# A weight tile place kept from the input stage, expert rows written back pair by pair, and a rearranged tail in a one-core transformer layer

## The chip, the core and the metric

The kernel runs on one core of a Trainium2 chip. The metric is device time in microseconds of one execution; the number compared is the median of repeated executions. One execution was recorded by the hardware profiler, and all rows below come from it.

## What is computed

One layer over 512 tokens of width 1024, all in float32: a modulated RMS norm, one wide input projection into a retention branch and a long convolution branch, a gated merge of both, an output projection with a residual, and then a mixture of experts. The experts hold most of the weights:

```python
h2 = modulate(rms_norm(x, norm2_g[layer]), sh2, sc2)
x = x + gt2 * moe_ffn(h2.reshape(-1, D_MODEL), *moe_args).reshape(x.shape)
return rms_norm(x, final_norm_g)

# moe_ffn: top-1 of 4 groups, top-2 of its 8 experts, and for each of 32 experts
def expert_block(args):
    xblk, e = args
    return (jax.nn.silu(xblk @ w1[e]) * (xblk @ w3[e])) @ w2[e]
```

Each of the 32 experts has `w1` and `w3` of 1024 x 512 and `w2` of 512 x 1024: 6 MB, 192 MB in all. That many bytes have to pass from HBM into the core once.

## The kernel before

The kernel works through the layer in stages. The first half (to about 548 us) is projections, retention and convolution; their weights are split into two parts on ScalarE and VectorE (`halved`), so TensorE makes three products for one. The normed tokens, eight tiles `hT` of [128, 2, 512], are an operand of every input projection; the last to read them is the second gate group, `gh` of `merge_group(1)`. After it come two more groups of that merge, `ho` (products with `hy_w_o`) and `ro` (with `ret_w_o`), and then the output projection (`w_out`), the residual and the router.

The second half is the expert stage. Experts are taken in 16 pairs. Each pair has a capacity of 64 tokens per expert, so a pair fills the 128 columns: expert 0 of the pair in the lower 64 partitions of a PSUM place, expert 1 in the upper. For a pair, TensorE does two `ga` and two `up` steps (`up_half`, L1536 to L1543, with `w1` and `w3`), the hidden product on ScalarE and VectorE (`hidden`), a transpose (`turned`, L1551) into `hT`, and two `y` steps (`down`, L1559) with `w2`. The result is scaled, split into `yh` and `yl`, and brought back to token order by products with the choice matrix `cmb` (`combine`, `add`, L1577 to L1590): for each of four token tiles and two halves of the width, the products are summed in PSUM and VectorE adds them to `xmid`.

Weights come in tiles of 1 MB, 12 to a pair: `plan` lists the 192 sources in the order of use, `sequence` the order of loading, and `ahead(n)` issues loads on SP, whose queue is worked in order. A tile goes to one of `NR` = 12 places of a ring (`ew`), or to a borrowed place (`loans`): work tiles of the expert stage that aren't needed yet (`cmb`, `hh`, `hT`, `y`, for tiles 6, 7, 10, 11), the tiles `xm` of the residual, and three spare ones (`xe0`, `xe1`, `xf`). From tile 16 on the pattern repeats every 16 tiles. A load waits until the products that read the place's last tile are done.

TensorE's order is written by hand in the expert stage (`tensor_order`); the order on SP, VectorE, ScalarE and GpSimd (POOL) is found by a planner, except in the tail (`with tc.manual_schedule()`), where all engines follow the text.

The loop over `g` in range(7) does two pairs per turn. The even pair's turn has `add(parts, places[:4])`, `turned`, `add(parts, places[4:])`, where `parts` holds the two pairs before; the odd pair adds nothing, but for `g == 6`. Pairs 14 and 15 stand behind the loop with their sums placed by hand: `fin` holds the first half of the width for four token tiles, `fin2` the second. In the last block the first half is added to `xmid` on VectorE, squared on ScalarE and multiplied by the final norm's gain on POOL (L1895 to L1899), and `leave` (from L1861) makes the norm, scales and sends out, two of the four rows on POOL (L1878).

Of the kernel before, what the change touches and what calls it, by code (L numbers as in the profile page):

```python
# [29 lines left out]
OV = 10  # L30
OA = 4
NA, NB, NC, NR, NW, NH = 12, 33, 4, 12, 2, 3
# [5 lines left out]
XE, XF = 12, 2  # L38
# [135 lines left out]
def body(es: ExitStack, tc: tile.TileContext, d, out, dump=None):  # L174
# [46 lines left out]
    rw = pa.tile([128, 8, 64], F32, name="rw")  # L221
    t1b = ExitStack()
# [649 lines left out]
    def start():  # L872
# [236 lines left out]

    def merge_group(ch):  # L1110
# [26 lines left out]

    gr, gh, ho, ro = merge_group(0)
# [17 lines left out]
    weave(ho, rest)  # L1156
    weave(ro, rest)
    run(rest)
    t1b.close()
# [10 lines left out]

    plan = []
    for p_ in range(16):
        for kc in range(2):
            for wt in ("w1", "w3"):
                for e in range(2):
                    plan.append(d[wt][2 * p_ + e, :, 4 * kc:4 * kc + 4, :].rearrange("p a b -> p (a b)"))
        for kc in range(2):
            for e in range(2):
                plan.append(d["w2"][2 * p_ + e, kc].rearrange("p a b -> p (a b)"))


    def borrow(pool, tag, bufs, units):
        def tile_():
            w = pool().tile([128, units, 512], F32, name="xw" + tag, tag=tag, bufs=bufs)
            return [w[:, u] for u in range(units)], w.rearrange("p a b -> p (a b)")
        return tile_

    lent_xm = [borrow(lambda: r2, "xm", 4, 2)] * 2
    wk_ = lambda: wk
    loans = {6: [borrow(wk_, "cmb", 4, 1)] * 4, 7: [borrow(wk_, "hh", HH, 1)] * 2 + [borrow(wk_, "hT", 2, 1)] * 2,  # L1190
             10: [borrow(wk_, "y", 4, 2)] * 2, 11: [borrow(wk_, "y", 4, 2)] * 2}
    sequence = [i for i in range(NR + len(loans)) if i not in loans] + list(LO)
    early_tiles = len(sequence)
    sequence += range(early_tiles, len(plan))

    loans.update((i, lent_xm) for i in range(early_tiles, len(plan) - 6)
                 if (i - early_tiles) % (NR + 4) < 2 and not 12 * OV + 8 <= i < 12 * OV + 8 + OA + 8)
    loans.update((i, [borrow(wk_, "xe0", 1, 2), borrow(lambda: late, "xe1", 1, 2)]) for i in range(early_tiles, len(plan) - 6)
                 if (i - early_tiles) % (NR + 4) == XE)
    loans.update((i, [borrow(wk_, "xf", 1, 4)]) for i in range(early_tiles, len(plan) - 6)  # L1200
                 if (i - early_tiles) % (NR + 4) == XF)
    PIECES = {len(plan) - 6: ((0, 2), (2, 3), (3, 4)), len(plan) - 4: ((0, 2), (2, 4)),
              len(plan) - 2: ((0, 2), (2, 3), (3, 4))}
    ready, lent = {}, {}
    issued, taken = [0], [0]

    def borrowed(src, places, queue=S):
        units = []
        for u, w in places:
            c0 = 512 * len(units)  # L1210
            queue.dma_start(w, src(slice(c0, c0 + 512 * len(u))))
            units += u
        return units

    def ahead(n):

        while issued[0] < min(n, len(plan)):
            i = sequence[issued[0]]
            src = plan[i]
            issued[0] += 1  # L1220
            if i in loans:
                if i < early_tiles and not lent:

                    lent.update((j, [place() for place in loans[j]]) for j in AL)
                ready[i] = borrowed(lambda c: src[:, c], lent.pop(i, None) or [place() for place in loans[i]])
                continue
            if i in PIECES:

                both = [ring_.tile([128, 4, 512], F32, name="ew", tag="ew") for e in range(2)]
                for a, b in PIECES[i]:  # L1230
                    for e, w in enumerate(both):
                        S.dma_start(w[:, a:b], plan[i + e].rearrange("p (a b) -> p a b", b=512)[:, a:b])
                for e, w in enumerate(both):
                    ready[i + e] = [w[:, u] for u in range(4)]
                issued[0] += 1
                continue
            w = ring_.tile([128, 2048], F32, name="ew", tag="ew")
            S.dma_start(w, src)
            ready[i] = [w[:, 512 * u:512 * u + 512] for u in range(4)]
# [50 lines left out]
    def prefetch():  # L1290
        for i in range(NR):
            yield
            ahead(i + 1)

    run(out_group(0, lambda o: [out_tile(o[m], m) for m in range(4)]))
    early, pre = early_steps(), prefetch()
# [406 lines left out]
    for g in range(7):  # L1703
# [7 lines left out]
        if g == 0:  # L1711
# [221 lines left out]
```

## Time and profile before

| | us |
|---|---|
| median of 3 runs (1096.97 to 1098.73) | 1098.47 |
| the profiled execution | 1098.42 |
| its span | 1096.8 |
| TensorE (PE) busy | 1056.1 |
| VectorE (DVE) busy | 580.1 |
| ScalarE (ACT) busy | 333.6 |
| bytes moved by DMA | 289.22 MB |

A reader begins with the slices of the span: in which stretch the DMA engines are full and in which TensorE has slack. Then come the waits of SP, which tell whether a stream of loads is held by its rate or by the places it loads into, and only then the order of instructions on TensorE in the stretch that matters. A share of busy time over the whole span says little here, since its two halves have different limits.

### The profile page before, as it was taken

The numbers are of one execution on the slowest core, as the hardware profiler recorded it, in microseconds if no ns is written. First come the engines' busy times: TensorE is split into PE (matmuls) and PEld (weight loads), VectorE is DVE, ScalarE is ACT, GpSimd is POOL, SyncE is SP. The second block draws the span as 40 slices with busy tenths as digits, with TensorE's granted clock in tenths as the row PEclk, the third lists the DMA queues.
The fourth block names the chain that finished last, engine by engine and source line by source line (L and its number), as shares of the span: only waits on it lengthen the run. The fifth ranks groups of instructions, "written<-read, shape, count | busy, mean of one in ns | idle before, by whom it ended". The sixth has DMA issues, their size and how long they took to land. (4 is left out here: it accounts for less than half of the span.)

```text
span 1096.8 us, 13058 instructions
## 1 busy us (share of the span) xinstructions
PE 1056.1 (96%) x4960; PEld 671.8 (61%) x4960; DVE 580.1 (53%) x1036; ACT 333.6 (30%) x582; POOL 49.2 (4%) x75
## 2 busy tenths in 40 slices
PE   9999999999999999999999999999998989999995
PEld 5667888877778777878788634444443534344332
DVE  4788895775475768976534443434331424334214
ACT  3676442445533554333324111101010110201012
POOL 0100000000000000000002000000000000000002
PEclk9999999999999999999998999999999999999998
DMA  7933444111122117785299989999999999999992
GB/s 278 293 110 97 134 135 132 58 58 58 58 86 68 55 42 272 249 270 187 81 404 409 363 324 419 416 417 418 416 417 418 415 419 416 417 418 417 417 398 87
DMA packets 64585, 289.22 MB, mean 264 GB/s; under 512 B 8196, under 2 KB 10372, under 8 KB 45062
## 3 DMA queue, kind: packets, MB, share of 16 engines
q1 hardware_dynamic: 59558, 274.50, 65.0%
q0 software_dynamic: 4960, 13.84, 3.7%
q8 instruction: 40, 0.66, 0.2%
q14 instruction: 27, 0.22, 0.1%
HBM read 288.05 MB, written 4.19 MB: 266 GB/s over the span
## 5 line engine op out<-in xcount | busy, mean ns | idle before, releaser
L198 DVE TENSOR_TENSOR wL<-raw,wH 128x512 fp32r<-128x512 f32 x142 | 97.0, 687 | 116.2 <-ACT wH L197 107.5
L197 ACT CAST wH<-raw 128x512 fp32r<-128x512 f32 x142 | 87.9, 621 | 206.4 <-PE ro L202 33.7
L1542 PE MATMUL up<-ew,xgm 128*64 128x512 f32 x440 | 118.5, 594 | 9.3 <-DMA ew<-w 9.3
L1548 DVE TENSOR_TENSOR hh<-hh,up 128x512 f32<-128x512 f32 x16 | 11.0, 687 | 170.1 <-PE up L1542 170.1
L1542 PE MATMUL ga<-ew,xgm 128*64 128x512 f32 x344 | 93.8, 594 | 4.9 <-DMA ew<-w 4.9
L1567 PE MATMUL y<-ew,hT 128*64 128x512 f32 x360 | 92.8, 595 | 1.9 <-DVE hT L1556 1.9
L1542 PEld LDWEIGHTS up<-ew,xgm 128*64 128x64 f32 x440 | 36.6, 137 | 76.4 <-issue 56.2
L1542 PEld LDWEIGHTS ga<-ew,xgm 128*64 128x64 f32 x344 | 29.6, 137 | 46.8 <-issue 36.8
L1492 ACT ACTIVATE xr<-xr,rs 128x512 f32<-128x512 f32 x15 | 10.8, 722 | 145.6 <-DMA xr<-rows,idx 145.5
L1567 PEld LDWEIGHTS y<-ew,hT 128*64 128x64 f32 x360 | 30.3, 137 | 40.4 <-issue 35.3
L1590 DVE TENSOR_TENSOR xmid<-xmid,co 128x512 f32<-128x512 f32 x60 | 40.5, 687 | 19.6 <-PE co L1582 19.1
L1547 ACT ACTIVATE hh<-ga 128x512 f32<-128x512 f32 x16 | 9.6, 598 | 122.7 <-PE ga L1542 117.3
L197 ACT CAST yh<-yv 128x512 fp32r<-128x512 f32 x30 | 18.5, 618 | 86.5 <-DVE yv L1573 75.8
L1582 PE MATMUL co<-yh,cmb 128*128 128x512 f32 x108 | 43.9, 406 | 0.0
L1573 DVE SCALAR_TENSOR_TENSOR yv<-y,wsl,gt 128x512 f32<-128x512 f32 x30 | 22.5, 749 | 38.3 <-PE y L1567 35.6
L1582 PE MATMUL co<-yl,cmb 128*128 128x512 f32 x108 | 42.4, 392 | 0.0
L342 DVE SCALAR_TENSOR_TENSOR acc<-adaw,scT,acc 128x1024 f32<-128x1024 f32 x28 | 35.7, 1282 | 11.4 <-DMA adaw<-ada 11.3
L1491 DVE TENSOR_SCALAR xr<-xr,rs 128x512 f32<-128x512 f32 x15 | 7.3, 487 | 51.9 <-DMA xr<-rows,idx 51.9
L1485 POOL DMA_INDIRECT xr<-rows,idx x15 | 15.4, 1029 | 359.8 <-DVE wsl L1532 348.3
L198 DVE TENSOR_TENSOR yl<-yv,yh 128x512 fp32r<-128x512 f32 x30 | 20.7, 691 | 17.4 <-ACT yh L197 17.3
L1497 ACT ACTIVATE xgm<-xg,sh2c,am2c 128x256 f32<-128x256 f32 (+1 forms) x36 | 16.6, 538 | 36.3 <-PE xg L1510 34.2
L1582 PEld LDWEIGHTS co<-yh,cmb 128*128 128x128 f32 x108 | 20.3, 188 | 11.5 <-issue 4.1
(486 smaller groups left out, 2385.9 us busy)
## 6 DMA issues: line engine op xcount, KB each, us to landing
ew<-w SPq DMA_DIRECT2D x141, 1024.0 KB, 17.4
raw<-w_in SPq DMA_DIRECT2D x52, 512.0 KB, 3.6
xwxm<-w SPq DMA_DIRECT2D x40, 512.0 KB, 13.8
adaw<-ada SPq DMA_DIRECT2D x32, 512.0 KB, 6.3
xwxf<-w SPq DMA_DIRECT2D x11, 1024.0 KB, 15.0
xwxe<-w SPq DMA_DIRECT2D x20, 512.0 KB, 18.7
adaw<-ada SPq DMA_DIRECT2D x32, 256.0 KB, 6.3
raw<-ret_w_o SPq DMA_DIRECT2D x8, 512.0 KB, 3.9
```

Of the source, the lines that this page charges most:

```text
L197: A.copy(h, src)
L198: V.tensor_tensor(out=l, in0=src, in1=f(h), op=ALU.subtract)
L342: V.scalar_tensor_tensor(out=acc[i], in0=w, scalar=scT[:, k, 0:1], in1=acc[i], op0=ALU.mult, op1=ALU.add)
L1485: G.indirect_dma_start(out=xr[j], out_offset=None, in_=rows, in_offset=bass.IndirectOffsetOnAxis(ap=idx, axis=0), bounds_check=511, oob_is ...
L1492: A.activation(xr[j][:, 512:1024], xr[j][:, 512:1024], AF.Copy, scale=rs)
L1497: A.activation(o, p, AF.Identity, bias=sh2c[:, k:k + 1], scale=am2c[:, k:k + 1])
L1542: T.matmul(ab_[i][64 * e:64 * e + 64], xg[k][:, c0 + 64 * e:c0 + 64 * e + 64], w[e][q], start=(k == 0), stop=(k == 7))
L1548: V.tensor_tensor(out=hh, in0=hh, in1=ab_[1], op=ALU.mult)
L1567: T.matmul(y_[kc][64 * e:64 * e + 64], hT_[:, 128 * k + 64 * e:128 * k + 64 * e + 64], w[e][k], start=(k == 0), stop=(k == 3))
L1573: V.scalar_tensor_tensor(out=yv, in0=y_[n], scalar=wsl, in1=gt2[:, ns], op0=ALU.mult, op1=ALU.mult)
L1582: T.matmul(p, cmb[:, 128 * t:128 * t + 128], y[j][:, ns], start=(start and i + j == 0), stop=(stop and i == len(parts) - 1 and j == 1))
L1590: V.tensor_tensor(out=xmid[:, t, ns], in0=xmid[:, t, ns], in1=p, op=ALU.add)
```

## The change

- `NR` goes from 12 to 8. The tokens `hT` of the first half get a pool of their own, `hw`, that stays open; weight tiles 0 to 3 and then four of every 16 tiles (offset `XH` = 3) are loaded into it, each tile as two places and so as two transfers of 512 KB.
- `plan`, `sequence`, `loans` and `ahead` move ahead of the merge stage, and `prefetch(4)` issues the first four tiles between the steps of `ho` and `ro` in `merge_group(1)`.
- In pair 0, scaling and transposing pair 1's tokens and the choice matrix of the next two pairs move from behind `down` to ahead of `turned`.
- Each pair is written back during the next: `add` in both halves of the loop, with one pair in `parts`.
- Up to the overflow branch (`a < OV`) no more than 12 x 10 + 8 = 128 tiles are asked for.
- In the tail, `started` brings the residual into PSUM by a product with the identity ahead of the sums. Pair 14's first half gets it for four token tiles; the second half's sums of pair 14 stand at other places in pair 15; two of the four sums of `y0` move behind the last `y` products; the multiplication by the gain moves from POOL to VectorE and reads PSUM; the scaling of rows 0 and 1 moves from POOL to ScalarE; all rows leave first half first.

```diff
-NA, NB, NC, NR, NW, NH = 12, 33, 4, 12, 2, 3
+NA, NB, NC, NR, NW, NH = 12, 33, 4, 8, 2, 3
-XE, XF = 12, 2
+XE, XF, XH = 12, 2, 3
+    hw = es.enter_context(tc.tile_pool(name="hw", bufs=1, side="right", reuse_waits="tile"))
...
-            hl = pb.tile([128, 2, 512], F32R, name="hT", tag="hT", bufs=8)
+            hl = hw.tile([128, 2, 512], F32R, name="hT", tag="hw", bufs=8)
...
+    loans.update((i, [borrow(lambda: hw, "hw", 8, 2)] * 2) for i in range(4))
+    period = NR + 8
+    sequence = [i for i in range(NR + len(loans)) if i not in LO] + list(LO)
...
+    loans.update((i, loans[0]) for i in range(early_tiles, len(plan) - 6) if XH <= (i - early_tiles) % period < XH + 4)
...
+    def prefetch(n):
+        for i in range(n):
+            yield
+            ahead(issued[0] + 1)
...
-    weave(ho, rest)
-    weave(ro, rest)
+    pre = prefetch(4)
+    weave(ho, rest, pre)
+    weave(ro, rest, pre)
     run(rest)
+    run(pre)
     t1b.close()
...
             hh = hidden(ab_)
+            scaled(rs[1], 1)
+            run(token_columns(xg, [1], 128))
             now = []
...
+            gt, more = rows_of(1)
+            run(more)
             hT_ = turned(hh)
...
-        parts = []
-        ahead(12 * a + early_tiles + 20)
-        parts.append((now[0][0], down(hT_, now[0][1], ahead_weights)))
+        ahead(min(12 * a + early_tiles + 20, 12 * OV + 8) if a < OV else 12 * a + early_tiles + 20)
+        parts = [(now[0][0], down(hT_, now[0][1], ahead_weights))]
...
         hh = up(a + 1, xg)
-        if g == 6:
-            add(parts, places)
-            parts = []
+        add(parts, places)
...
-        parts.append((now[1][0], down(hT_, now[1][1], ahead_weights)))
+        parts = [(now[1][0], down(hT_, now[1][1], ahead_weights))]
...
+    def started(p, parts, t, n, residual=True):
+
+        if residual:
+            T.matmul(p, ident, xmid[:, t, cols[n]], start=True, stop=False)
+        combine(parts, t, n, p, not residual, False)
...
+    p = bank("hT")
+    fin, fin2 = [bank("fin") for t in range(3)], []
+    started(fin[0], parts, 0, 0)
+    some(step, 1)
     hh = hidden(ab_)
+    started(fin[1], parts, 1, 0)
+    started(fin[2], parts, 2, 0)
     hT_ = turned(hh, p)
     ahead(len(plan))
-    y = down(hT_, now[0][1], ahead_weights, lambda: combine(parts, 2, 0, fin[2], True, False))
     fin.append(bank("fin"))
-    combine(parts, 3, 0, fin[3], True, False)
+    started(fin[3], parts, 3, 0)
+    y = down(hT_, now[0][1], ahead_weights)
...
-    some(step, 2)
+    some(step, 1)
+    fin2.append(bank("fin", "acc"))
+    T.matmul(fin2[0], ident, xmid[:, 0, cols[1]], start=True, stop=False)
     more_sums(yn[0], 0, fin[0])
     more_sums(yn[0], 1, fin[1])
     some(step, 1)
     more_sums(yn[0], 2, fin[2])
     more_sums(yn[0], 3, fin[3])
...
-    second_half()
-    second_half()
-    some(step, 1)
+    more_sums(yn[1], 0, fin2[0])
+    some(step, 2)
     hh = hidden(ab_)
     early_table(AF.Sqrt, hh[:, 0:1])
+    fin2.append(bank("fin", "acc"))
+    T.matmul(fin2[1], ident, xmid[:, 1, cols[1]], start=True, stop=False)
     hT_ = turned(hh, bank("hT", "acc"))
+    more_sums(yn[1], 1, fin2[1])
...
         A.copy(yh, yv)
+        fill()
         V.tensor_tensor(out=yl, in0=yv, in1=f(yh), op=ALU.subtract)
...
-            if t < 2:
-                G.tensor_scalar(out=o, in0=o, scalar1=r, scalar2=None, op0=ALU.mult)
-            else:
-                A.activation(o, o, AF.Copy, scale=r)
+            A.activation(o, o, AF.Copy, scale=r)
...
-        for t in range(4):
+        def first_half(t):
             more_sums(y0, t, fin[t], True)
-            x_ = xmid[:, t, cols[0]]
-            V.tensor_tensor(out=x_, in0=x_, in1=fin[t], op=ALU.add)
-            square(t, 0, x_)
-            G.tensor_tensor(out=o_[0][:, t], in0=x_, in1=fn[:, cols[0]], op=ALU.mult)
+            square(t, 0, fin[t])
+            V.tensor_tensor(out=o_[0][:, t], in0=fin[t], in1=fn[:, cols[0]], op=ALU.mult)
+
+        first_half(0)
+        first_half(1)
         last_products(ys1, w[1], (2, 3))
-        y1 = last_scaled(1, ys1)
+        y1 = last_scaled(1, ys1, lambda: first_half(2))
+        first_half(3)
```

## Rows read from the trace of the kernel before

**Rows 1.** The page's slices, 40 equal parts of the span: rate of all transfers

```profile
GB/s 278 293 110 97 134 135 132 58 58 58 58 86 68 55 42 272 249 270 187 81 404 409 363 324 419 416 417 418 416 417 418 415 419 416 417 418 417 417 398 87
```

**Rows 2.** Stretches of the span: length, each engine's busy us (instructions), PE clock, DMA share, GB/s

```profile
585.00:600.00 15.00, 14.67 (x84) 13.39 (x83) 9.39 (x24) 7.04 (x15) 2.81 (x6) 0.81 1.02 406
...
600.00:617.00 17.00, 16.18 (x133) 14.17 (x133) 11.04 (x38) 3.34 (x7) 3.21 (x4) 0.97 0.98 386
...
641.00:648.00 7.00, 6.42 (x34) 2.81 (x36) 4.26 (x15) 1.25 (x3) 2.46 (x2) 1.00 0.54 146
...
700.00:1040.00 340.00, 322.87 (x1530) 142.39 (x1528) 115.26 (x217) 40.80 (x70) 12.40 (x14) 1.00 1.02 417
```

**Rows 3.** What SP waited for from 614 to 660 us: us, times, longest

```profile
SPq L1238 <- PE ga L1542: 12.9, 2, 10.3
...
SPq L1238 <- PE y L1567: 9.6, 1, 9.6
```

**Rows 4.** SP's instructions in time order: start, us, line, count; loads of weight tiles

```profile
646.31 0.80 SPq L1238 DMA_DIRECT2D ew<-w  x2
...
662.94 0.80 SPq L1238 DMA_DIRECT2D ew<-w  x2
...
733.07 1.59 SPq L1211 DMA_DIRECT2D xwxm<-w  x2
...
735.59 0.33 SPq L1211 DMA_DIRECT2D xwxf<-w  x1
...
738.09 0.33 SPq L1238 DMA_DIRECT2D ew<-w  x1
```

**Rows 5.** TensorE in time order, pairs 0 and 1: start, us, line, out<-in, count

```profile
628.04 0.61 PE L1477 MATMUL wsl<-wHL,gtm 128*128 128x8 f32 x4
...
631.50 3.65 PE L1567 MATMUL y<-ew,hT 128*64 128x512 f32 x16 [1.04 <-DVE hT L1556]
...
642.63 3.65 PE L1542 MATMUL ga<-ew,xgm 128*64 128x512 f32 x16
```

**Rows 6.** The same, with VectorE: end of `up` to `y` in pairs 1, 2 and 13

```profile
656.51 1.53 PE L1510 MATMUL xg<-ident,xr 128*128 128x128 f32 x12
...
659.26 7.09 PE L1567 MATMUL y<-ew,hT 128*64 128x512 f32 x32 [0.17 <-DVE hT L1556]
...
680.01 0.50 PE L1582 MATMUL co<-yh,cmb 128*128 128x512 f32 x1
...
689.71 3.65 PE L1567 MATMUL y<-xwxm,hT 128*64 128x512 f32 x16
...
1004.63 0.50 PE L1582 MATMUL co<-yh,cmb 128*128 128x512 f32 x1
...
1005.41 4.86 DVE L1590 TENSOR_TENSOR xmid<-xmid,co 128x512 f32<-128x512 f32 x8
...
1011.84 7.09 PE L1567 MATMUL y<-ew,hT 128*64 128x512 f32 x32 [0.28 <-DVE hT L1556]
```

**Rows 7.** The chain of waits, last 36 us: start, us, engine, tile, line, count

```profile
1060.87 0.86 PE fin L1823 x2
...
1061.73 0.46 PE fin L1582 x2
...
1076.46 2.04 PE fin L1778 x8
...
1081.88 1.68 DVE yl L1854
```

**Rows 8.** All engines in time order, pair 15 and the tail

```profile
1049.56 1.02 PE L1542 MATMUL up<-ew,xgm 128*64 128x512 f32 x2
...
1051.11 3.65 PE L1542 MATMUL up<-ew,xgm 128*64 128x512 f32 x14 [0.53 <-DMA ew<-w]
...
1074.57 0.69 DVE L1854 TENSOR_TENSOR yl<-yv,yh 128x512 fp32r<-128x512 f32 x1 [0.69 <-ACT yh L1853]
...
1077.99 5.01 POOL L1899 TENSOR_TENSOR o<-xmid,fn 128x512 f32<-128x512 f32 x4 [61.58 <-DVE xmid L1897]
```

More of the change, by code (lines that the diff above doesn't have):

```diff
@@ L1108, in body, with borrow, tile_ @@
     rest = rest_of_modulation()
+    plan = []
+    for p_ in range(16):
+        for kc in range(2):
+            for wt in ("w1", "w3"):
+                for e in range(2):
+                    plan.append(d[wt][2 * p_ + e, :, 4 * kc:4 * kc + 4, :].rearrange("p a b -> p (a b)"))
+        for kc in range(2):
+            for e in range(2):
+                plan.append(d["w2"][2 * p_ + e, kc].rearrange("p a b -> p (a b)"))
+    def borrow(pool, tag, bufs, units):
+        def tile_():
+            w = pool().tile([128, units, 512], F32, name="xw" + tag, tag=tag, bufs=bufs)
+            return [w[:, u] for u in range(units)], w.rearrange("p a b -> p (a b)")
+        return tile_
@@ new lines, in body @@
+    loans.update((i, lent_xm) for i in range(early_tiles, len(plan) - 6)
+                 if (i - early_tiles) % period < 2 and not 12 * OV + 8 <= i < 12 * OV + 8 + OA + 8)
+    loans.update((i, [borrow(wk_, "xe0", 1, 2), borrow(lambda: late, "xe1", 1, 2)]) for i in range(early_tiles, len(plan) - 6)
+                 if (i - early_tiles) % period == XE)
+    loans.update((i, [borrow(wk_, "xf", 1, 4)]) for i in range(early_tiles, len(plan) - 6)
+                 if (i - early_tiles) % period == XF)
@@ new lines, in body, with borrowed @@
+    loans.update((i, loans[0]) for i in range(early_tiles, len(plan) - 6) if XH <= (i - early_tiles) % period < XH + 4)
+    PIECES = {len(plan) - 6: ((0, 2), (2, 3), (3, 4)), len(plan) - 4: ((0, 2), (2, 4)),
+              len(plan) - 2: ((0, 2), (2, 3), (3, 4))}
+    ready, lent = {}, {}
+    issued, taken = [0], [0]
+    def borrowed(src, places, queue=S):
+        units = []
+        for u, w in places:
+            c0 = 512 * len(units)
+            queue.dma_start(w, src(slice(c0, c0 + 512 * len(u))))
+            units += u
+        return units
@@ new lines, in ahead @@
+    def ahead(n):
+        while issued[0] < min(n, len(plan)):
+            i = sequence[issued[0]]
+            src = plan[i]
+            issued[0] += 1
+            if i in loans:
+                if i in AL and not lent:
+                    lent.update((j, [place() for place in loans[j]]) for j in AL)
+                ready[i] = borrowed(lambda c: src[:, c], lent.pop(i, None) or [place() for place in loans[i]])
+                continue
+            if i in PIECES:
+                both = [ring_.tile([128, 4, 512], F32, name="ew", tag="ew") for e in range(2)]
+                for a, b in PIECES[i]:
+                    for e, w in enumerate(both):
+                        S.dma_start(w[:, a:b], plan[i + e].rearrange("p (a b) -> p a b", b=512)[:, a:b])
+                for e, w in enumerate(both):
+                    ready[i + e] = [w[:, u] for u in range(4)]
+                issued[0] += 1
+                continue
+            w = ring_.tile([128, 2048], F32, name="ew", tag="ew")
+            S.dma_start(w, src)
+            ready[i] = [w[:, 512 * u:512 * u + 512] for u in range(4)]
@@ L1169, in body @@
         S.dma_start(xm[i], d["xT"][i])
[L1171 to L1239, printed above, removed]
@@ L1288, in early_steps @@
             yield
[L1290 to L1293, printed above, removed]
     run(out_group(0, lambda o: [out_tile(o[m], m) for m in range(4)]))
-    early, pre = early_steps(), prefetch()
+    early, pre = early_steps(), prefetch(NR)
     last, use_ = fm_products(8, mixed, "wo")
@@ L1909, in body @@
         fin2[3] = x_
-        V.scalar_tensor_tensor(out=wk.tile([128, 512], F32, name="junk3", tag="cmb", bufs=4), in0=x_, scalar=1.0, in1=x_,
+        V.scalar_tensor_tensor(out=xr[1][:, 512:1024], in0=x_, scalar=1.0, in1=x_,
                                op0=ALU.mult, op1=ALU.mult, accum_out=fs[:, 1, 3:4])
```

37 lines of the change are left out of this document (15 added, 22 removed).

## The prediction, made before the change was run

> **What bounds the kernel now.** First the busy time by stretch [rows 1, 2]. From 700 us to 1040 us the core's DMA engines move 417 GB/s at a full DMA share while TensorE is busy 322.87 of 340 us: the expert stage is a DMA stage with a TensorE close behind, 17.1 us of slack over some 11.3 pairs, 1.5 us a pair. Just before, the same view has a hole: 641 to 648 us at 146 GB/s. Next, what the DMA queue's engine (SP) waits for between 614 and 660 us [rows 3]: 12.9 us for TensorE's `ga` products (10.3 of it on end) and 9.6 us for its `y` products. A wait for products is a wait for a buffer. So at 641 us every place for a weight tile was full, and the stream went on at 646.31 us [rows 4], when the first step of pair 1 (642.63 + 3.65) [rows 5] had read its two tiles. The end follows from there: remaining bytes over rate, then a tail in which the last products, sums and norms run one after the other [rows 7, 8].
>
> The sum is made against the profiled execution, 1098.42 us with a span of 1096.8; the median of the three runs, 1098.47, is the same for this purpose.
>
> **Part 1, four weight tiles early.** 4 MB would take 4 x 2.5 = 10 us (a whole tile is 738.09 - 735.59 = 2.50 us in the issue times [rows 4]). They move into a stretch with an idle DMA (the slices before 548 us [rows 1]). But there is no new room: the ring shrinks from 12 to 8 tiles, the kept place holds 4, and every period of 16 tiles reuses the same places at the same distance. Before 617 us the stream was already running at 386 to 406 GB/s [rows 2] and then stood for want of places. Loading earlier makes it stand earlier; it restarts when pair 1's first step ends, as now. Value 0; bounds 0 and -10 (what 4 tiles are worth if places were not the limit). A loss is possible only in part 1's own loads, a rival below.
>
> **Part 2, order in pair 0.** The transposes of pair 1's tokens move ahead of `turned`. Now TensorE goes from 628.04 to 642.63 us in 14.6 us [rows 5], and `y` (631.50) started late because the hT copy waited on VectorE. Transposes (0.85), slot sums and choices (1.7) and hT (0.45) end at 631.05 in the new order; VectorE has the hidden product, four column copies, two `cmb` copies and the hT copy ahead of `y`, about 4.9 us from 628.2, or 1.3 more if `gtm` gets in front: `y` starts at 633.2 to 634.4. Then 7.05 of `y` and 1.7 of choices: pair 1 at 641.9 to 643.2 against 642.63. The stream's restart moves by -0.7 to +0.6; value 0.
>
> **Part 3, half-tile loads.** A tile in the kept place is two places of 512 KB, so two transfers with 4 KB rows. From 16 to 185, 11 periods hold 4 such tiles, less what runs past the start's slack: 40 tiles on the stream's critical stretch. Two halves are issued in 735.59 - 733.07 = 2.52 us (`xwxm` x2) against 2.50 for a whole one [rows 4]: 0.02 us a tile, 0.8 in all. From above: the stretch with the smallest pieces, 585 to 600 us, ran at 406 instead of 417 GB/s [rows 2], 2.6%, 0.066 us a tile, 2.6 in all. I take 0.03, nearer to the row of the same size: +1.2. The Trainium skill (SBUF — State Buffer, "The DMA setup-cost knee") speaks against splitting: each transfer pays about 2 us, coalesce; if the 40 additional transfers paid it in the open, that would be an estimated +80 us. Halves following each other at full share say that here it lies behind other transfers, so it is left out.
>
> **Part 4, rows written back every pair.** TensorE does the same products; VectorE does 8 more additions per two pairs, and each stands where a PSUM place must come free. Pair 13 already does this: from its last `up` to `y` 1011.84 - 1004.63 = 7.2 us, against 659.26 - 656.51 = 2.75 in odd pair 1 [rows 6]: +4.46. The even pair now spends 689.71 - 680.01 = 9.7 us; 16 of 32 sum products at 0.46 / 2 = 0.23 [rows 7] go, 3.7, but eight additions (4.86 [rows 6]) plus the hidden product, the hT copy and what follows them set a floor near 7.0: it saves 2.7 to 3.7. Net +0.8 to +1.8 per two pairs, 0.4 to 0.9 a pair, under the slack of 1.5: hidden. Exposed only in pair 1, where places are still full: its `y` releases the next place 4.46 later than 662.94 [rows 4]; from 646.3 eight tiles last until 666.4, slack 3.5, so 0 to 1.0 of standing, and half-places come free half a step earlier. Value +0.3. The new bound on tiles ahead of the overflow branch issues four tiles one step later with more than ten ahead of use: 0.
>
> **Part 5, the tail.** Pair 14 gets four residual products at 0.86 [rows 7], +3.4; between the last two steps of pair 15 two second halves (2 x (0.86 + 0.46) = 2.7) go and one (1.3) comes earlier: +2.0 us of work until the last `up`. Against that stand the waits it fills: `up` at 1049.56 did 2 products, stood until 1051.11 and took 3.65 for 14 [rows 8], where 16 take 3.65 [rows 5]: some 1.5 in all. I estimate 0.8 more from switching and later weights. Net -0.3, bounds -2.3 (further waits filled) and +2.0 (none). After it, 4 of 8 sums (2.04 / 2 = 1.0 [rows 7]) leave the path for VectorE's and ScalarE's time: -1.0. The last `yl` took 1.68 [rows 7], the one before 0.69; POOL's four multiplications ran from 1077.99 for 5.01 us beside the long one [rows 8]. They go to VectorE in a gap: -1.0, or 0 if it is not POOL. The Trainium skill (SBUF — State Buffer, "Who interferes with whom") says a VectorE operation with two inputs in SBUF can be shut out by a GpSimd one reading SBUF; by that rule the 1.0 is gained, without it the tail gives 1.3. Scaling rows 0 and 1 on ScalarE instead of POOL puts them before a square, and the outputs leave in turn: 0, one pass of 0.69 either way. Tail -2.3, bounds -4.3 and 0.7.
>
> **Sum:** 0 + 0 + 1.2 + 0.3 - 2.3 = -0.8; 1098.4 - 0.8 = **1097.6 us**. Not all bounds fall on one side; its own range is 1094.2 to 1101.5.
>
> **The rivals.**
> 1. The early tiles count in full: the places are not what stops the stream. Then it ends 10 us sooner, and TensorE, 1.5 us a pair behind, keeps most of it: about -8, 1090. For it: DMA at full share to the end [rows 2]. Against it: the waits of [rows 3], which are for products, not for landings. 0.12.
> 2. The tail gains more: the residual sums of pair 14 sit wholly in waits. -2.0 more, 1095.6. Against it: the fourth needs the PSUM place that the hT copy frees, so TensorE still stands there. 0.10.
> 3. Slower: writing back every pair makes TensorE the bound. It decides when two pairs cost over 3.0 us more (twice the slack). If VectorE's additions eat all of the even pair's saving, 4.46 remain: 1.46 too much, over 5.5 double pairs +8.0, less the tail: 1105; at half the saving lost, +3: 1101. For it: TensorE 95% busy [rows 2]. Against: the even pair's sums run at 0.23 a product and most of them stay ahead of VectorE. 0.13.
> 4. The early loads queue in front of the merge stage's own weights: four tiles are 10 us, and products stand if more than three lie ahead of one load, about +2.5 once: 1100.1. They wait on SP for the last `gh` products to have read the tokens, and the loads of `ret_w_o` stand behind them. Against: they are asked for one per step. 0.07.
> 5. The change doesn't load early: the SP order puts the four behind the later loads. By part 1 nothing else moves: 1097.6. 0.08.
>
> **How the numbers follow.** Forecast 0.50: 0.36 of it within 0.2% (2.2 us, what a measurement here can tell from no change), 0.10 faster, 0.04 slower. Rivals 1 and 2 are faster, 0.22; of rival 5, 0.02 faster, 0.06 same; rival 3 slower, 0.13; of rival 4, 0.05 slower, 0.02 same. Faster 0.34, same 0.44, slower 0.22. The range leaves out rival 1 and the worst of 3: 1093.5 to 1102.
>
> **What would show it.** Part 1: four kept tiles landing before 548 us, the DMA standing before 617 us, and the restart still at the end of pair 1's first step, near 646 us; a restart earlier than 644 makes part 1 wrong. Part 3: GB/s from 700 to 1040 us a little under 417. Part 4: odd pairs 7.2 us from `up` to `y`, even ones near 7, TensorE idle still left before 1000 us. Part 5: no POOL in the last 20 us, the last `yl` at 0.69. If the last landing comes over 3 us sooner or later, the stream's account is what failed.

## The result: 0.64% slower, and two effects that no step had counted

| | before | after |
|---|---|---|
| median of 4 runs each, us | 1098.32 | 1104.89 |
| lowest to highest, us | 1096.97 to 1098.73 | 1104.32 to 1106.22 |
| ratio, 95% interval | | 1.0064 (1.0046 to 1.0081) |
| profiled execution: time, span, us | 1098.42, 1096.8 | 1104.39, 1102.8 |

The forecast was 1097.6 us with a range to 1102.0; the kernel became slower by more than the range allowed. First the lines of after that answer to the rows of before. Its stretches (length; busy us of PE, PEld, DVE, ACT, POOL; PE clock; DMA share; GB/s) beside [rows 2], and the stretch in which the stream stands:

```profile
635.00:645.00 10.00, 8.99 (x28) 2.71 (x30) 1.71 (x3) 0.59 (x1) 0.00 (x0) 0.66 0.33 110
...
700.00:1040.00 340.00, 328.67 (x1532) 138.93 (x1530) 134.82 (x257) 42.06 (x72) 12.46 (x14) 0.98 1.02 414
```

What SP waited for from 616 to 666 us [rows 3]:

```profile
SPq L1155 <- PE ga L1550: 15.2, 4, 12.7
SPq L1182 <- PE y L1575: 14.6, 1, 14.6
```

SP's issues in time order [rows 4], the first of the early loads:

```profile
490.14 0.33 SPq L1155 DMA_DIRECT2D xwhw<-w  x1
498.75 0.38 SPq L1155 DMA_DIRECT2D xwhw<-w  x1
505.77 0.90 SPq L1155 DMA_DIRECT2D xwhw<-w  x2
```

TensorE in pairs 0 and 1 [rows 5], with the end of `up` to `y` in pair 1 [rows 6]:

```profile
636.01 6.66 PE L1575 MATMUL y<-ew,hT 128*64 128x512 f32 x16 [2.15 <-DVE hT L1564]
...
647.94 3.65 PE L1550 MATMUL ga<-ew,xgm 128*64 128x512 f32 x16
...
661.82 0.50 PE L1590 MATMUL co<-yh,cmb 128*128 128x512 f32 x1
...
669.07 4.08 PE L1575 MATMUL y<-xwhw,hT 128*64 128x512 f32 x17 [0.27 <-DVE hT L1564]
```

VectorE in the tail, the last `yl` [rows 8] and the product that POOL had:

```profile
1088.64 0.68 DVE L1861 TENSOR_TENSOR yl<-yv,yh 128x512 fp32r<-128x512 f32 x1
1089.24 0.68 DVE L1903 TENSOR_TENSOR o<-fin,fn 128x512 f32<-128x512 f32 x1
```

To see where 6.0 us of span come from, take the time of the same event in both profiles, one event after the other, and note by how much the delay of after grows between two of them:

| from, to | before | after | delay grows by |
|---|---|---|---|
| start of the span to `ssT` | 16.40 | 25.33 | +8.9 |
| to the first `wo` | 540.5 | 544.8 | -4.6 |
| to `cum` | 604.2 | 606.2 | -2.3 |
| to the first `ga` of pair 0 | 614.2 | 616.2 | 0 |
| to the first `ga` of pair 1 | 642.6 | 647.9 | +3.3 |
| to delivery of weight tile 28 | 648.1 | 653.6 | +0.2 |
| to delivery of tile 189 of 192 | 1062.2 | 1070.4 | +2.7 |
| to the end of the span | 1096.8 | 1102.8 | -2.2 |

(Tiles are counted in the DMA records, by the bytes landed. The time given for tile 28 is that of the first bytes that land behind the first 28 MB, so it is the restart of the stream.) The first of these events, in before and in after:

```profile
16.40 0.95 PE L910 MATMUL ssT<-pick,ssr 128*128 128x1 f32 x8
```

```profile
25.33 0.95 PE L912 MATMUL ssT<-pick,ssr 128*128 128x1 f32 x8
```

The largest two terms lie in the first half, where the prediction had nothing change but the loads of rival 4. The -2.3 ahead of `cum` goes with a stretch at half clock, 594 to 601 us in before [rows 2], that doesn't lie there in after; a stretch as long, 6.8 us, lies in pair 0 there (the clock 0.66 above). The last two terms are read on the stream. Read on TensorE, by the first `ga` of pair 14 (1018.7 and 1025.2 us) in place of tile 189, they are +1.0 and -0.5.

### The profile page after: what moved, and what is told of

It is laid out like the page before. It is cut to its first block, busy times and chain, and to the rows that moved or that the text cites. A ratio compares the mean times of both kernels' runs of the same rounds, so it can differ in the third digit from the quotient of the medians.

```text
span 1102.8 us, 13182 instructions
## 1 busy us (share of the span) xinstructions
PE 1060.0 (96%) x4968; PEld 665.4 (60%) x4968; DVE 601.6 (55%) x1084; ACT 334.2 (30%) x584; POOL 41.2 (4%) x69
## 5 line engine op out<-in xcount | busy, mean ns | idle before, releaser
L1550 PE MATMUL up<-ew,xgm 128*64 128x512 f32 x312 | 85.1, 593 | 1.6 <-DMA ew<-w 1.6
L1575 PE MATMUL y<-ew,hT 128*64 128x512 f32 x232 | 68.3, 633 | 2.1 <-DVE hT L1564 2.1
L1598 DVE TENSOR_TENSOR xmid<-xmid,co 128x512 f32<-128x512 f32 x108 | 66.3, 681 | 5.3 <-PE co L1590 5.3
L1550 PE MATMUL ga<-ew,xgm 128*64 128x512 f32 x216 | 61.4, 593 | 1.4 <-DMA ew<-w 1.4
L1550 PE MATMUL up<-xwhw,xgm 128*64 128x512 f32 x128 | 54.1, 593 | 0.3 <-DMA xwhw<-w 0.3
L1550 PEld LDWEIGHTS up<-ew,xgm 128*64 128x64 f32 x312 | 26.2, 137 | 39.0 <-issue 34.7
L1590 PE MATMUL co<-yh,cmb 128*128 128x512 f32 x108 | 46.5, 430 | 0.0
L1575 PE MATMUL y<-xwhw,hT 128*64 128x512 f32 x128 | 42.7, 595 | 1.1 <-DVE hT L1564 1.1
L1575 PEld LDWEIGHTS y<-ew,hT 128*64 128x64 f32 x232 | 20.5, 145 | 28.3 <-issue 25.3
L1550 PEld LDWEIGHTS ga<-ew,xgm 128*64 128x64 f32 x216 | 18.9, 137 | 25.8 <-issue 23.1
## 6 DMA issues: line engine op xcount, KB each, us to landing
ew<-w SPq DMA_DIRECT2D x93, 1024.0 KB, 13.8
```

The costliest lines, as they stand in the source:

```text
L1550: T.matmul(ab_[i][64 * e:64 * e + 64], xg[k][:, c0 + 64 * e:c0 + 64 * e + 64], w[e][q], start=(k == 0), stop=(k == 7))
L1575: T.matmul(y_[kc][64 * e:64 * e + 64], hT_[:, 128 * k + 64 * e:128 * k + 64 * e + 64], w[e][k], start=(k == 0), stop=(k == 3))
L1590: T.matmul(p, cmb[:, 128 * t:128 * t + 128], y[j][:, ns], start=(start and i + j == 0), stop=(stop and i == len(parts) - 1 and j == 1))
L1598: V.tensor_tensor(out=xmid[:, t, ns], in0=xmid[:, t, ns], in1=p, op=ALU.add)
```

## The experiments

Each was timed beside the kernel before on its own chip; ratios are against that.

### What makes POOL stand at the start

The first row that differs is POOL's first selection. Before, then after, POOL in time order, each with the sequencer's line that belongs to it (POOLq: count; min/median/max ns; first and last start):

```profile
1.55 0.29 POOL L208 TENSOR_SCALAR_AFFINE_SELECT ident<-ident 128x128 f32<-128x128 f32 x1 [0.29 <-POOL ones L211]
...
L208 POOLq MODIFY_POOL_CONFIG  x2: 11/11/11, 1.5 to 1.5; - x2
```

```profile
1.06 0.20 POOL L211 MEMSET ones<- 128x128 f32 x1
11.79 0.29 POOL L208 TENSOR_SCALAR_AFFINE_SELECT ident<-ident 128x128 f32<-128x128 f32 x1 [10.53 <-issue]
...
L208 POOLq MODIFY_POOL_CONFIG  x2: 11/11/11, 1.3 to 1.3; - x2
```

The same instruction, at the same place in the program, starts 10.2 us later, after an idle time of 10.5 us for which the profile shows no releaser. In both kernels POOL's sequencer changes its configuration just ahead of it; in before the selection follows within 0.1 us, in after 10.5 us later. `ident` is needed by ScalarE's first step, and `ss` and all that follows by that.

**e1_tail_alone**: the kernel before, everything from `ahead(12 * 14 + ...)` on taken from after. **e2_no_tail**: the reverse.

> The kernel before with only the tail of the changed kernel (sums spread, no POOL multiplications, ScalarE scales all rows); places, loads, pair 0 and write-back as before. Theory A: the 10.5 us for which POOL stands ahead of its first selection in the changed kernel (1.26 to 11.79 us, against 1.26 to 1.55 before) come with the tail's edit, which takes POOL's only multiplications out of the program. Then this kernel shows the stand too: first selection at 11.8 us, first ga of pair 0 about 2.0 us late (616.2 for 614.15), and the tail 2.4 us shorter, so 1098.3 + 2.0 - 2.4 = 1097.9 us. Theory B: the stand belongs to another part of the change or to nothing in it: first selection at 1.55 us and 1098.3 - 2.4 = 1095.9 us. From the delivery of the last weight tile to the end of the span both expect 29.7 us for 32.1.

> The changed kernel with the old tail (POOL's multiplications and scalings back), its other parts kept. Theory A (the start's stand comes with the tail): first selection of POOL at 1.55 us, first ga of pair 0 near 614.2, delivery of the last tile to the end 32.1, so 1104.9 - 2.0 + 2.4 = 1105.3 us. Theory B (it does not): first selection at 11.8 us and 1104.9 + 2.4 = 1107.3 us.

Measured: 1105.77 us, ratio 1.0081 (1.0068 to 1.0094), the selection at 11.98; and 1097.10 us, ratio 1.0002 (0.9993 to 1.0010), the selection at 1.55. The stand comes with the tail's edit, which lies a thousand us behind it in the program. Its price was misjudged in both texts: the 2.0 us at pair 0 was a net of two things. Alone it puts the first `ga` at 622.2 us (+8.1) and the span up by 8.6, the tail's gain included. "POOL's only multiplications", in e1's text, is not right for after: that kernel has three POOL products of 128x512, at 271, 298 and 384 us, ahead of its first broadcast.

**e5_mult_behind**: after, with one POOL product behind the last broadcast:

```diff
         G.partition_broadcast(fn[:, 512 * j:512 * j + 512], row)
+    G.tensor_tensor(out=junk2, in0=fn[:, 1023:1024], in1=fn[:, 1022:1023], op=ALU.mult)
```

> The changed kernel with one more POOL instruction: a product of 128x1 elements right behind the last broadcast, 60 us ahead of the end, of a kind that the old tail also put there; nobody reads it. The runs without the old tail's POOL work all stand some 10.5 us ahead of POOL's first selection, the run with it does not. Theory: what POOL was last made to do in one execution decides whether the next execution stands at its first selection, so this product takes the stand away: first selection at 1.5 us, first ga of pair 0 near 607, time 1095.7 us (1097.1 of the run with the old tail less 1.4 for the shorter work from pair 14's first step to the end, 77.6 us for 79.0). Rival: the stand comes from the tail's other edits or from how the program is laid out; then it stays at 11.8 us and the time at 1104.9.

Measured: 1095.48 us, ratio 0.9981 (0.9969 to 0.9992): 9.1 us less than after by the ratios, from one 128x1 product whose result nobody reads. POOL in time order, start and end of e5:

```profile
1.55 0.29 POOL L208 TENSOR_SCALAR_AFFINE_SELECT ident<-ident 128x128 f32<-128x128 f32 x1 [0.29 <-POOL ones L211]
...
1013.63 1.46 POOL L1777 PARTITION_BROADCAST fn<-xr  x2 [4.71 <-DMA xr<-fnorm]
1022.41 0.18 POOL L1778 TENSOR_TENSOR junk<-fn 128x1 f32<-128x1 f32 x1 [7.32 <-issue]
```

The stand has not gone, it has moved: 7.3 us behind the broadcast, where nobody waits for POOL. In before the old tail's multiplications did the same service inside a wait of 61.58 us [rows 8]. The sequencer's line for them in before, and the first broadcast in after:

```profile
L1899 POOLq MODIFY_POOL_CONFIG  x2: 127/127/127, 1016.3 to 1016.4; - x2
```

```profile
621.23 1.48 POOL L1678 PARTITION_BROADCAST gt<-mrow  x2 [6.55 <-issue]
```

Such a change of configuration stands in three places and no others: ahead of the first selection, ahead of the first broadcast, and ahead of a product that follows the last broadcast, where the program has one. The first broadcast stands 6.1 to 7.6 us in all 17 profiles. The selection stands 10.5 to 11.1 us in after, e1, e3 and e4, the four kernels without POOL work behind the last broadcast, and starts at 1.55 us in the other 13. So what counts is not whether a program has POOL products, since after has three, but whether one comes behind the last broadcast. That an edit at the end acts on the start through the execution before, in which POOL's last work was the broadcast, is inferred from this and from e1, e2 and e5; no trace holds two executions. The Trainium skill (GPSIMD Engine Reference, "Instruction dispatch") says that the first call to a freshly loaded piece of POOL code costs some 6 us with no visible instruction; the runs agree in kind, with 6.6, 7.3 and 10.5 us.

### Why 4.6 us come back

From `ssT` to the first `wo` TensorE is busy nearly throughout in both kernels, yet after needs 4.6 us less. Products on the normed tokens (`v`, `gr`, `gh`, `qk`, `g`) follow each other at 227 ns in after, e2, e3 and at 231 to 235 in before, e1, e4; `wo` takes 227 and `ro` 234 in all six. Only the tokens' place differs. **e6_shift32**: the kernel before, with

```diff
     sm = t1b.enter_context(tc.tile_pool(name="sm", bufs=1, side="right"))
+    pad = sm.tile([128, 8], F32, name="pad")
```

> The kernel before with one unused tile of 32 bytes a partition ahead of the tiles on the right side, so that the normed tokens and the other tiles of the first half lie 32 bytes further; nothing else. In the runs with kept places the products on the normed tokens follow each other at 227 ns, without them at 234 (v, gr, gh, qk, g), while wo takes 227 and ro 234 in all of them: where both operands of a product start at the same remainder by 64 bytes it is 227, where not 234. Theory: the remainder is the cause; here all products of hy, qk, v, g, gr, gh, ho and ro go at 227, the first wo begins 5.5 to 7 us sooner (540.5 before) and the whole shift reaches the end: 1097.1 - 7 = 1090 us, down to 1088 with what ho and ro add. Rival: it is the place at the far end of the memory or what lies beside it; then 234 ns and 1097.1.

Measured: 1091.41 us, ratio 0.9939 (0.9922 to 0.9956), first `wo` at 532.8 for 540.5. One line each of `gr`, `ro` and `wo` (count; min/median/max ns of one; first and last start); before, then e6, then after:

```profile
L201 PE MATMUL gr<-hT,wH x64: 389/396/502, 351.5 to 480.3; 128*128 128x512 f32 x64
...
L201 PE MATMUL ro<-retH,wH x64: 393/396/502, 435.0 to 539.8; 128*128 128x512 f32 x64
...
L201 PE MATMUL wo<-mixed,wH x64: 387/389/479, 540.5 to 589.8; 128*128 128x512 f32 x64
```

```profile
L201 PE MATMUL gr<-hT,wH x64: 387/389/499, 346.6 to 473.5; 128*128 128x512 f32 x64
...
L201 PE MATMUL ro<-retH,wH x64: 389/389/499, 428.9 to 532.1; 128*128 128x512 f32 x64
...
L201 PE MATMUL wo<-mixed,wH x64: 387/389/479, 532.8 to 582.3; 128*128 128x512 f32 x64
```

```profile
L201 PE MATMUL gr<-hT,wH x64: 387/389/499, 357.4 to 485.0; 128*128 128x512 f32 x64
...
L201 PE MATMUL ro<-retH,wH x64: 391/395/497, 440.2 to 544.1; 128*128 128x512 f32 x64
```

The median of one product falls from 396 to 389 ns, by the same 7 ns as the distance from one to the next, and only where the tokens' start moved against the weights'. After gains less than e6 because in it only the places of `hT` moved: `ro` stays at 395 ns. **e15_shift96** (`[128, 24]` for `[128, 8]`) asks which remainder counts.

> As the run with the 32-byte tile ahead of the first half's tiles, with a tile of 96 bytes. With 32 bytes the normed tokens and the weight halves start at the same remainder by 64, 128 and 256 bytes; with 96 they agree by 64 alone (by 128 it is 32 against 96). If the remainder by 64 bytes decides, the products of gr and ro follow each other at 227 ns again; if that by 128 or more, at 234, and the time is that of the kernel before.

Measured: 1096.72 us, ratio 0.9997 (0.9982 to 1.0013), and

```profile
L201 PE MATMUL gr<-hT,wH x64: 391/394/496, 350.5 to 479.3; 128*128 128x512 f32 x64
...
L201 PE MATMUL ro<-retH,wH x64: 393/396/501, 434.0 to 538.8; 128*128 128x512 f32 x64
```

So agreement by 64 bytes doesn't suffice, and the theory quoted for e6 is corrected by this: the products are fast where both operands start at the same remainder by at least 128 bytes. (In these kernels such operands agree by 256 bytes too, so no run tells 128 from 256.) In the program of before the tokens lie at remainder 0 and the weight halves at 96; in after and e6 both at 96; in e15 at 32 and 96. `mixed` lay at 96 all along. One product of e15 is outside the rule: `v`, in which the weight halves are the moving operand, goes at 229 ns there, for 232 to 235 in before and 227 in e6, while `gr`, `gh`, `qk` and `g` stay at 233 to 235. So the rule is not the whole of it.

### Pair 0

**e3_pair0_old** takes part 2 back in after; **e8_mult_pair0** does so in e5; **e13_shift32_pair0** puts part 2 alone into e6; **e14_rows_behind_hT** leaves in e5 all of part 2 but one step:

```diff
-            gt, more = rows_of(1)
-            run(more)
             hT_ = turned(hh)
+            gt, more = rows_of(1)
+            run(more)
```

> The changed kernel with pair 0's order as before: the second half's scaling, its turned columns and the next rows stand behind the first pair's y again. Theory: the 3.3 us that pair 0 lost (first ga of pair 0 to first ga of pair 1 31.7 us against 28.4) come from that order, because VectorE's product for the next rows (1.28 us) stands ahead of the copy of hT and TensorE's wait there is followed by a first y at the half clock (6.66 us for 3.65). Then that distance is 28.4 again, the first y takes 3.65 us, and the time is 1104.9 - 3.3 = 1101.6 us. Rival: the half clock in the first y comes from the later start of pair 0 (2.0 us) and not from the order; then it stays somewhere in pair 0 and the time is 1104 to 1105.

> The changed kernel with the POOL product behind the last broadcast and with pair 0's order as before. Against the run that has the product alone it tells what that order costs when nothing stands at the start. Theory: the order itself is neutral (first ga of pair 0 to first ga of pair 1 28.5 us with the old order, 28.8 with the new one where no half clock falls into either); what made 31.7 of it was a stretch at the half clock, which costs 2 to 3 us in the first y and also 2.3 us where it falls ahead of cum. So within 1 us of the run with the product alone, with 28.5 us and the half clock's stretch elsewhere. Rival: the order costs the whole 3.3 us; then 3.3 us faster than the run with the product alone.

> The kernel before with the 32-byte shift (1091.4 us) and pair 0's new order, nothing else. On the changed kernel the new order was worth 1095.5 for 1092.6 us, +2.9, of which the profiles show +0.3 as order and the rest as a stretch at the half clock in the first y (in three of the four profiles with the new order, in none of the seven with the old). Theory: the order brings that stretch into the first y, so it costs 2 to 3 us here too: 1093.5 to 1094.5, with 30 us or more from the first ga of pair 0 to the first ga of pair 1. Rival: the +2.9 hung on what lay around it in the changed kernel; then 1091.4 within 1 us and 28.5 us.

> The changed kernel with the POOL product (1095.5 us) and one step of pair 0's new order taken back: the rows of the next pairs (VectorE's product of 1.28 us and what goes with it) are set up behind the copy of hT and not ahead of it; the scaling and the turned columns of the second half keep their new place ahead of the first y. Theory: the wait of 2.15 us that VectorE's queue puts ahead of the first y is what the half clock follows; without it y begins 1.3 us sooner, at its full clock, and the time is near that of the old order, 1092.6 to 1093.5. Rival: the wait has no part in it (the transposes and small products that stand there have); then 1095.5 less 1.3 at most, 1094.2 or more, with the half clock still in y.

| | ratio (interval) | first `ga` of pair 0 to that of pair 1 | first `y` |
|---|---|---|---|
| e3, old order | 1.0075 (1.0059 to 1.0091) | 28.7 | full clock |
| e5, new order | 0.9981 (0.9969 to 0.9992) | 30.4 | half clock |
| e8, old order | 0.9958 (0.9941 to 0.9974) | 28.5 | full |
| e14, new but rows behind | 0.9949 (0.9933 to 0.9965) | 29.3 | half |
| e6, old order, old places | 0.9939 (0.9922 to 0.9956) | 28.5 | full |
| e13, new order, old places | 0.9937 (0.9920 to 0.9953) | 28.8 | full |

e13 settles one half: with the old places the new order is neutral (0.3 us in pair 0, none in the time), though TensorE waits 2.15 us there too. e3 was inconclusive: its gain in pair 0 was eaten, 2.4 us by a half clock that fell ahead of `cum` again (610.2), 1.8 ahead of the first `wo`, where another 3.4 us at half clock lie at 30.5 us. In the changed kernel the whole order costs 2.5 us (e5 against e8, the intervals overlap by a little), and taking back one of its steps is worth 3.5 (e5 against e14, they don't). So e8's theory, that the order is neutral, has fallen, and its rival's 3.3 is near. The first `y` of e13, then of e14:

```profile
626.94 3.65 PE L1568 MATMUL y<-ew,hT 128*64 128x512 f32 x16 [2.15 <-DVE hT L1557]
```

```profile
626.46 5.35 PE L1575 MATMUL y<-ew,hT 128*64 128x512 f32 x16 [0.95 <-DVE hT L1564]
```

The longer wait has the full clock behind it and the shorter one the half clock. So "the half clock follows the wait", the theory for e14, has fallen as a mechanism although its time came out (1092.99 us). What the profiles show is a pattern: with new order and kept places the half clock lies in the first `y` in four of four (after, e2, e5, e14), with new order and old places in none of two (e4, e13), with the old order in none of eleven. Why the kept places matter for it is open. The pattern rests on one profiled execution of each kernel, and executions of one kernel differ in this: e11's six took 1088.81 us (mean granted clock 0.991) to 1096.28 us (0.985).

### Early tiles, half tiles, write-back

**e4_old_places** is after with the loads and places of before. **e9_whole_tiles** is e8 with two tokens sharing a place of a whole tile, so that it is loaded by one transfer; **e11_whole_pad** is e9 with the 32-byte tile; **e10_two_pairs** is e8 with `if g == 6:` ahead of the write-back again.

> The changed kernel with the places and loads of before: twelve ring places of 1 MB tiles, no kept places, no half-tile loads with 4-KB rows, no four early tiles; pair 0, write-back and tail as changed. Theory: the half-tile loads cost 2.9 us between the restart of the stream and its end (419.5 us for 416.6), and the early tiles nothing. Then the stretch is 416.6 to 417.0 again and the time is 1104.9 - 2.9 = 1102.0 us, with the first y of pair 0 still at the half clock. Rival 1: the 2.9 us come from the write-back by pairs; then 1104.9. Rival 2: the early tiles were worth something after all and their loss shows: over 1104.9.

> The changed kernel with the POOL product behind the last broadcast and pair 0's old order (that is the last run, 1092.6 us), and with the eight half-tile places kept for the normed tokens as four places of a whole tile: two tokens share a place, and each of the 24 tiles loaded into them is one transfer of 1 MB with 8-KB rows. Theory: the 4-KB rows of the 96 half-tile transfers cost about 2 us of the 2.8 us by which the stream from tile 28 to tile 189 is longer than with the old places and the old write-back (414.3 us in the mean of four runs, 417.1 in five). Then the stretch is 415 us and the time 1090.6. Rival: rows of 4 KB cost nothing here and the write-back by pairs or the order of the places does it; then 417 and 1092.6.

> The changed kernel with the POOL product and pair 0's old order (1092.6 us), and with the write-back after every two pairs as before. Theory: the write-back by pairs lies under the slack of the weight stream (prediction: 0.3 us; the run with old places and new write-back showed 415.1 us of stream against 414.3, so at most 0.8): 1092.0 to 1092.6. Rival: it is what makes the stream longer; then 1090.

> As the run with whole-tile places, and the 32-byte tile ahead of the other tiles of the first half, so that the products of ho, ro and the inverse transforms go at 227 ns for 234 too (hy, qk, v, g, gr and gh already do). Theory: some 350 products by 6 to 7 ns are 2.2 us, all of it reaching the end: 1090.6 - 2.2 = 1088.4 us. Rival: what is gained ahead of pair 0 is lost in where the half clock falls; then 1090.6.

Measured ratios: e4 1.0107 (1.0091 to 1.0124); e9 0.9977 (0.9967 to 0.9986); e10 0.9959 (0.9946 to 0.9972); e11 0.9945 (0.9925 to 0.9964); to be read against after (e4), e8's 0.9958 (e9, e10) and e9 (e11). e4's text was wrong by 7 us: with the old places the gain on the normed tokens goes too, which it had not seen (first `wo` at 550.6); its second rival, over 1104.9, has the number but not the reason. e10 equals e8: the write-back by pairs costs nothing. e9 is the miss that teaches. The stretch of [rows 2] in e8, then in e9:

```profile
700.00:1040.00 340.00, 328.21 (x1516) 138.55 (x1514) 132.61 (x253) 39.38 (x68) 12.61 (x15) 0.98 1.02 414
```

```profile
700.00:1040.00 340.00, 328.43 (x1521) 138.70 (x1517) 135.03 (x257) 40.75 (x70) 12.62 (x15) 0.98 1.02 417
```

With whole tiles the stream runs at 417 GB/s again, 415.5 us from tile 28 to 189 for 417.6, as expected. Yet the time isn't better; by the ratios it is 2 us worse, with intervals that overlap. Two reasons stand in the profiles. Pair 0 starts 3.4 us later (610.9 for 607.5; 1.7 from a longer half clock behind the last `wo`, and 1.5 ahead of the first, for which the record shows no cause). And at the end the gain is not used: the tiles of pair 14's first `ga` are there 5.6 us ahead of it in e9, 4.1 in e8, 3.4 in after.

The waits of TensorE from 700 to 1060 us (us in total, times, longest) show why, in before and then in after:

```profile
PE up L1542 <- DMA ew<-w: 9.3, 9, 1.4
PE ga L1542 <- DMA ew<-w: 4.9, 4, 1.4
...
PE wsl L1477 <- DVEq L1605: 1.3, 1, 1.3
```

```profile
PE wsl L1485 <- PEq L1613: 6.2, 1, 6.2
...
PE up L1550 <- DMA ew<-w: 1.6, 2, 1.3
PE ga L1550 <- DMA ew<-w: 1.4, 1, 1.4
```

In before TensorE waits 14 us for weight tiles, up to 1051 us; in after 3 us, the last time at 915 us (in e9 at 906). Behind that TensorE sets the time, and the chain of work that ended last has no DMA in it in after, in before 29%. Two things go with this. TensorE's path is longer with the write-back of every pair: pairs 2 to 8 take 167.0 us in the nine kernels that do it, 162 to 164 in the others. And `wsl` at the overflow branch stands 6.2 to 6.4 us in these nine, with 10.2 us at half clock that begin inside this stand, at 914 to 939 us by the kernel; in the eight others it stands 1.3 us and that stretch is missing. Why the branch costs more is not shown. e10, with the old write-back in e8's kernel, waits 15.3 us for tiles instead, the last time at 966 us, and takes the same time.

e11 was expected 2.2 us under e9 and is 3.5 under it by the ratios.

### The tail, and a kernel that beats both

**e12_tail_mult** is before with the new tail and the POOL product; **e7_shift32_tail** is that with the 32-byte tile.

> The kernel before with the changed tail and the POOL product behind the last broadcast, nothing else: the tail's own price. The prediction gave it -2.3 us; with the 32-byte shift on both sides it measured 1089.07 for 1091.41, that is -2.3, while the profiles showed 77.4 us for 78.2 from pair 14's first step to the end. Theory: -2.3 by the timed runs, 1094.9; rival: only the 0.4 to 0.8 of the profiled stretch, 1096.4 to 1096.8; the tail's stand returning would be 1105.8.

> The kernel before with three things: the 32-byte shift, the changed tail, and the POOL product of 128x1 behind the last broadcast. Places, loads, pair 0 and write-back as before. If the stand is taken away by the product and the tail is worth 0.4 us (77.6 us from pair 14's first step to the end for 78.0), 1090 - 0.4 = 1089.6 us; if the tail is worth the 2.3 us that the prediction gave it, 1087.7; if the stand stays, 1098.5.

e12: 1097.43 us, ratio 0.9992 (0.9982 to 1.0002). e7: 1089.07 us, ratio 0.9919 (0.9905 to 0.9933), for e6's 0.9939. And e5 stands to e2 as 0.9981 to 1.0002. By these three pairs the new tail is worth 0.9, 2.2 and 2.3 us; the intervals of the first two pairs overlap. e12's 0.9 for the 2.3 of its text, with an interval that holds 1, is a miss; e7 came out between the two figures of its text. e7 is the fastest kernel of the study, 0.8% under before: of the change it keeps the tail alone.

## Why the prediction was wrong

**Part 1, right.** The eight half-tiles were issued from 490 to 511 us; the DMA then ran out of places sooner, 110 GB/s from 635 to 645 us; tile 28 came 5.7 us behind pair 1's first `ga`, in before 5.5. Loading earlier made the stream stand earlier. Rivals 1 and 5 fell with it; rival 4 did not show in after, no product waited in the merge stage.

**Part 2, right as an order, wrong in this kernel.** `y` did get behind VectorE's product, 19.8 us from the first `ga` for 17.3, and e13 shows +0.3 us, inside -0.7 to +0.6. The working had no term for TensorE's clock, though 585 to 600 us stood at 0.81 in [rows 2]: a stretch at the lower of its two levels (1.2 for 2.4 GHz) lies ahead of `cum` in before (-2.3) and in the first `y` of pair 0 in after (6.66 us for 3.65, +3.0). e2 and e5 show both, so "it moved" is a reading of two profiles.

**Part 3, mis-sized, then covered.** From tile 60 to tile 189 after takes 334.0 us and before 331.8; all seven profiles with half tiles lie between 333.8 and 334.1, all ten without between 331.7 and 332.0. 2.1 us over 8 periods of 4 tiles is 0.066 us a tile. The text chose 0.03, from the row of the same size, over 0.066, from [rows 2]: the upper bound was the value. With whole tiles in the same places e9 takes 332.0 us for e8's 334.1, so it is the halves and not the places. That the share of the packets in a full queue counts, and not the issue of two transfers, is argued and not shown. By the Trainium skill (SBUF — State Buffer, "The DMA setup-cost knee") it would have been 2 us for each additional transfer, if paid in the open; the trace shows a thirtieth of that. Little of it reaches the end, because from 916 us on TensorE sets the time.

**Part 4, right in time, wrong in what is left behind it.** Odd pairs take 7.1 to 7.3 us from `up` to `y` (669.07 - 661.82 in pair 1), even ones 6.9, as expected, and e10 finds no cost in the time. But the slack is used up: of the 14 us that TensorE waited for tiles in before, 3 are left. Rival 3's mechanism, TensorE as the bound, holds from 916 us on; its price, 2.6 to 6.6 us more than before, does not.

**Part 5, right in size in two of three pairs, wrong in what belongs to it.** The last `yl` took 0.68 us, and the tail is worth 0.9, 2.2 and 2.3 for the forecast 2.3. The step that failed is "POOL off": taking POOL's work out of the tail (the multiplications, counted as a gain of 1.0 at 1078 us, and the scaling of two rows, counted at 0) was priced by the tail alone. It was also the last thing that POOL did in an execution, and without it the next one starts 8.9 us late. No view of one execution shows that; [rows 8] show only that POOL had work there.

**The range.** The parts' upper bounds add up to +4.9 (0.6, 2.6, 1.0, 0.7), 1103.3; the 1101.5 of the sum isn't worked out. The tail's own terms give +2.0 - 1.0 = +1.0 at most, not 0.7. The measured 1104.89 lies outside all of these.

**What was missing.** Two terms, +8.9 and -4.6 us, both side effects: what POOL did last in the execution before, and where a tile comes to lie. With them the forecast would have been 1097.6 + 4.3 = 1101.9. The other 2.5 us to the profiled 1104.4 lie in places where it had terms: by the table pair 0 with the clock 3.3 - 2.3 = 1.0, the restart 0.2, the stream 2.7 for 1.5 (parts 3 and 4), the tail -2.2 for -2.3. The last two agree as arithmetic and not as causes, since TensorE and not the stream sets the time there; by pair 14's `ga` they are +1.0 and -0.5. Rival 3's price (1101 to 1105) was met by the time by luck: what makes the kernel slower is POOL's stand at the start.

## What to carry to other kernels

When an edit takes an engine's last work out, compare what that engine does last with what it does first: executions follow each other, and a 128x1 product in a slack place was worth 9 us here. When an edit moves a tile, compare the start addresses of both operands of every product that reads it by 128 bytes; 32 bytes were worth 6 us. Line up the same event in both profiles from the start of the span, not from the edited code. And before a gain in the stream is counted, look which engine sets the time at the end.

## What the hardware showed that was not expected

- POOL stands 10.5 us ahead of a selection (at the start, in the kernels whose last POOL work is a broadcast), 6.6 us ahead of the first broadcast of after, or 7.3 us ahead of a product behind a broadcast in e5. At each of these places the profile shows a change of configuration by POOL's sequencer, and nothing that takes the time.
- Products of 128x512 in the split format follow each other at 227 ns when both operands start at the same remainder by 128 bytes, at 231 to 235 ns otherwise, but for `v` in e15, with 229 at remainders 96 and 32.
- A stretch of 3.4 or 6.8 us at the half clock lies between 586 and 655 us in all profiles but one (e4), at places that differ. From the last `wo` to `cum` it takes 11.6 us without it, 12.3 with 3.4 us of it, 13.8 to 14.0 with 6.8, the same to 0.2 us in all 17 profiles.
- A stretch of 10.2 us at the half clock begins inside TensorE's stand of 6.2 to 6.4 us at the overflow branch in all nine profiles with write-back by pairs, and is missing in the eight others, which stand 1.3 us there.
- With four of every 16 tiles loaded as two halves of 512 KB, the stream of 700 to 1040 us runs at 414 GB/s instead of 417.
